# A column mean over 8192 rows: the last row group split 4, 4, 2 and 1 blocks, seven blocks loaded early, five stores

## Chip, cores and metric

One core of a Trainium2 chip. The time is device microseconds from launch to end. Before the change five runs gave a median of 628.69 us (628.66 to 628.92). The core has a matrix engine (TensorE, PE in the profile), which adds over the partitions here; a vector engine (VectorE, DVE); ScalarE (ACT) and GpSimd (POOL); and SyncE (SP), which only issues transfers and waits. Matmul results are held in PSUM, everything else in SBUF, with 128 partitions each.

## The reference

```python
def setup_inputs():
    return {
       "x": np.random.randn(8192, 8192).astype(np.float32),
    }

def reference(x: np.ndarray) -> np.ndarray:
    return np.mean(x, axis=0)
```

The input is 256 MiB of float32, the output 8192 numbers.

## The kernel before

The 8192 rows are 64 groups of 128, one row per partition. A group is 8192 columns wide, 16 blocks of 512 (`F`). The sum over the rows has two parts. First VectorE adds groups elementwise into an accumulator `acc` of 128 x 8192. Then TensorE adds over the partitions: a matmul with a 128 x 32 matrix `ones`, whose entries are 1/8192, leaves the mean of its columns in 32 partitions of PSUM, all alike. Four such matmuls write to the four quarters of a PSUM tile (partitions 0, 32, 64 and 96). Several matmuls accumulate in the same place, so that the late groups need not pass through `acc`: TensorE adds them in directly.

The buffers are six rows of one SBUF tile `bufs`. Rows 0 to 3 take loads in turn, row 4 is `both`, row 5 is `acc`. All loads are issued by SyncE in program order (line 75, in the helper `load`) and share one queue; a load into a buffer waits for the operation that last read it. `load_rows` loads several groups with one transfer.

The order is this. `head` takes 3 blocks of group 60 ahead of time and `ahead` 4 blocks of group 63. Groups 0 to 3 and 4 to 5 come in two large loads. Groups 6 to 53 come in pairs: one load for two groups, one add of the two into `both`, one add of `both` into `acc` (lines 118 to 123). Groups 54 to 59 come one by one, with one add each. Of group 60 only blocks 3 to 15 are loaded and added, of group 61 all are loaded and blocks 5 to 15 added (line 129). Group 62 is loaded, and GpSimd adds its blocks 13 to 15 to `acc` (line 136). Group 63 comes in three loads: blocks 0 to 7, 12 and 13, 14 and 15 (line 139).

An add in the helper `add` (line 95) that waits both for a load and for the add ahead of it does so through a no-op on ScalarE or GpSimd (line 98), which waits for both and releases VectorE.

The table `plan` (line 142) gives the order of the matmuls (line 169) on TensorE: `ahead`, the blocks of `acc` as they become final, the parts of groups 61, 60, 62 and 63 that are not in `acc`. The blocks 0 to 11 go to three PSUM tiles `banks`, four blocks each. Blocks 12 and 13, and 14 and 15, go in pieces of 256 columns to two smaller tiles `ends`.

Results leave PSUM by a copy to SBUF: ScalarE copies `banks[2]`, `banks[0]`, `banks[1]` and `ends[0]` (line 183), VectorE copies `ends[1]` (line 201). Four stores follow (line 186): one of blocks 8 to 11 on ScalarE's queue, one of blocks 0 to 7 on SyncE's, one of 12 and 13 on ScalarE's and one of 14 and 15 on SyncE's. The helper `landed` puts a no-op on SyncE (line 70) that waits for certain transfers, before the stores and behind them. VectorE's last no-op `hold` (line 212) waits for the store of blocks 0 to 7.

Of the kernel before, what the change touches and what calls it, by code (L numbers as in the profile page):

```python
# [9 lines left out]
def kernel(  # L10
# [32 lines left out]
    W = F // 2  # L43
    WHOLE = 12
# [11 lines left out]
    ahead = sb.tile([P, 4 * F], f32, name="ahead")  # L56
# [6 lines left out]
    banks = [psp.tile([P, F], f32, name=f"bank{b}") for b in range(3)]  # L63
    ends = [psp.tile([P, W], f32, name=f"end{e}") for e in range(2)]
# [20 lines left out]
    def rows(g, n=1):  # L85
        return x[g * P:(g + n) * P, :]
# [6 lines left out]
    def add(dst, a, b, dmas):  # L93

        ins = nc.vector.tensor_add(out=dst, in0=a, in1=b).ins  # L95
        if dmas and adds:
            waiter = nc.scalar if len(adds) % 8 > 1 else nc.gpsimd
            nop = joins[waiter] = tc.keep_in_program_order(waiter.nop()).ins  # L98
            for o in dmas + adds[-1:]:
                tc.add_manual_dep(nop, o.name, sync, reason="the no-op waits")  # L100
            for group in ("loads", "adds"):
                tc.declare_no_dep(ins, group=group, reason="the no-op waited")
            tc.add_manual_dep(ins, nop.name, sync, reason="waits for both at once")
        elif adds:
            tc.declare_no_dep(ins, group="loads", reason="the add ahead waited")
        tc.add_to_no_dep_group("adds", ins)
        adds.append(ins)

    head = sb.tile([P, 3 * F], f32, name="head")
    load(head[:], rows(G - 4)[:, :3 * F])  # L110
    first, second = load_rows(0, 0, 4), load_rows(4, 4, 2)
    load(ahead[:], rows(G - 1)[:, 8 * F:WHOLE * F])
# [3 lines left out]
    tc.keep_in_program_order(nc.scalar.copy(out=warm[:], in_=ones[:]))  # L116
    g = 6
    while g < G - 10:
        u = (g + 2) % 4
        dma = load_rows(g, u, 2)  # L120
        add(both, bufs[:, u, :], bufs[:, u + 1, :], [dma])
        add(acc, acc, both, [])
        g += 2
# [5 lines left out]
    for lo, loaded in [(3, 3), (5, 0)]:  # L129
        row = bufs[:, (g + 2) % 4, :]  # L130
        dma = load(row[:, loaded * F:], rows(g)[:, loaded * F:])
        add(acc[:, lo * F:], acc[:, lo * F:], row[:, lo * F:], [dma])
        g += 1
    r61, r62, r63 = [bufs[:, (g + 1 + j) % 4, :] for j in range(3)]
    load(r62, rows(g))
    tc.keep_in_program_order(nc.gpsimd.tensor_add(  # L136
        out=acc[:, 13 * F:], in0=acc[:, 13 * F:], in1=r62[:, 13 * F:]))
    g += 1
    for lo, hi in [(0, 8), (12, 14), (14, 16)]:
        load(r63[:, lo * F:hi * F], rows(g)[:, lo * F:hi * F])  # L140

    plan = [
        (ahead, 8, 12),
        (acc, 3, 5),
        (acc, 0, 3),
        (r61, 0, 5),
        (head, 0, 3),
        (acc, 5, 12),
        (r62, 0, 12),
        (r62, 12, 13),  # L150
        (acc, 12, 14),
        (acc, 14, 16),
        (r63, 0, 8),
        (r63, 12, 14),
        (r63, 14, 16),
    ]
    sums = []
    for row, lo, hi in plan:
        base = 8 * F if row is ahead else 0
        if lo < WHOLE:  # L160
            for i in range(lo, hi):
                cols = row[:, i * F - base:(i + 1) * F - base]
                sums.append((banks[i // 4], i % 4, cols))
        else:
            for c in range(lo * F, hi * F, W):
                e, q = divmod(c // W - 2 * WHOLE, 4)
                sums.append((ends[e], q, row[:, c:c + W]))
    for n, (dst, q, cols) in enumerate(sums):
        tc.keep_in_program_order(nc.tensor.matmul(  # L169
            out=dst[32 * q:32 * q + 32, :],  # L170
            lhsT=ones[:],
            rhs=cols,
            start=all(d is not dst or k != q for d, k, _ in sums[:n]),
            stop=all(d is not dst or k != q for d, k, _ in sums[n + 1:]),
            tile_position=(0, 32 * q),
            skip_group_check=True,
        ))

    res = both[:, :3 * F].rearrange("p (b c) -> p b c", b=3)
    tails = [both[:, 3 * F:3 * F + W], tail[:]]  # L180

    def copy(dst, src):
        tc.keep_in_program_order(nc.scalar.copy(out=dst, in_=src))  # L183
# [7 lines left out]
    def end(e):  # L191
        return (out[(WHOLE + 2 * e) * F:(WHOLE + 2 * e + 2) * F].rearrange("(q c) -> q c", q=4),
                tails[e][0:P:32, :])

    copy(res[:, 2, :], banks[2][:])
    s2 = store(nc.scalar, out[8 * F:12 * F].rearrange("(q c) -> q c", q=4), res[0:P:32, 2, :],
               loads[-3])
    for b in range(2):
        copy(res[:, b, :], banks[b][:])
    copy(tails[0], ends[0][:])  # L200
    nc.vector.tensor_copy(out=tails[1], in_=ends[1][:])  # L201
# [4 lines left out]
    s01 = store(nc.sync, out[:8 * F].rearrange("(b q c) -> q b c", b=2, q=4), res[0:P:32, 0:2, :])  # L206
    s3 = store(nc.scalar, *end(0))
    store(nc.sync, *end(1))
    landed(loads[-2], s2)
    landed(loads[-1], adds[-1])  # L210
    landed(s01, s3)
    hold = tc.keep_in_program_order(nc.vector.nop()).ins
    tc.add_manual_dep(hold, s01.name, sync, reason="VectorE ends late")
# [30 lines left out]
```

## Time and profile before

| What | us |
|---|---|
| median of 5 runs | 628.69 |
| the profiled execution, its own time | 628.67 |
| its span, first to last instruction | 626.8 |
| VectorE busy | 526.1 (84%) |
| TensorE busy | 17.5 (3%) |
| GpSimd, ScalarE busy | 4.0, 3.5 |
| load stream, over the span | 428 GB/s |
| last load landed | 623.07 |

The page has a row for each engine over the span cut into 40 slices, each digit a busy share in tenths, and a row for the sixteen transfer engines together. Groups of instructions are named by line, engine, operation and tile, with their number, busy time and mean; behind a bar stands how long the engine was idle before them and what ended that. The chain of waits follows the work that ended last back from its end. In the timeline a row gives start and length. SPq and ACTq are the sequencers of SyncE and ScalarE, where a transfer is issued. PEld is TensorE's loading of weights, and each float32 matmul shows as two records.

### The profile page before, as it was taken

The page shows a single profiled execution, that of the slowest core. Times are in us where ns is not written, and L with a number is a line of the kernel's source. Part 1 is how long each engine was busy: PE and PEld are TensorE (multiplying, and loading weights), DVE is VectorE, ACT ScalarE, POOL GpSimd, SP SyncE. Part 2 cuts the span into 40 slices and gives each one's busy share as a digit, 9 for nine tenths or more (in the row PEclk, how much of TensorE's full clock was granted, in tenths as well). Part 3 has the DMA queues.
Part 4 walks back from the last instruction along what each step waited for, and adds up shares of the span by engine and source line. Part 5 has one row for each costly group of instructions (what it writes and reads, how often), then busy time and mean ns, then how long its engine had stood idle before and what let it go on. Part 6 is the DMA issues. An engine that isn't in the chain of part 4 may idle for free.

```text
span 626.8 us, 475 instructions
## 1 busy us (share of the span) xinstructions
PE 17.5 (3%) x124; PEld 4.7 (1%) x124; DVE 526.1 (84%) x60; ACT 3.5 (1%) x6; POOL 4.0 (1%) x7
## 2 busy tenths in 40 slices
PE   0000100000000000000000000000000000000027
PEld 0000000000000000000000000000000000000002
DVE  0028999999888998888988889888898888999991
ACT  0000000000000000000000000000000000000001
POOL 0000000000000000000000000000000000000002
PEclk9999999999999999999999999999999999999999
DMA  9999999999999999999999999999999999999997
GB/s 385 460 410 412 458 452 418 443 427 435 435 418 452 402 468 402 468 402 468 402 468 402 468 402 468 402 456 414 448 422 443 427 435 412 425 435 435 439 425 294
DMA packets 5926, 268.50 MB, mean 428 GB/s; under 512 B 656, under 2 KB 664, under 8 KB 1060
## 3 DMA queue, kind: packets, MB, share of 16 engines
q1 hardware_dynamic: 5908, 268.46, 99.2%
q8 instruction: 1, 0.02, 0.0%
q10 hardware_dynamic: 16, 0.01, 0.0%
q14 instruction: 1, 0.01, 0.0%
HBM read 268.44 MB, written 0.03 MB: 428 GB/s over the span
## 4 chain that ended last, share of the span: by engine, by line
DMA 56%; DVE 33%; another core or an unknown queue 10%; issue 0%; SPq 0%; PE 0%; ACTq 0%; POOLq 0%; POOL 0%
DMA bufs<-in_x_dram 56%; DVE bufs L95 33%; SPq L75 0%; PE end L169 0%; ACTq L98 0%; DVE tail L201 0%; POOLq L98 0%; POOL ready L62 0%; POOL ones L59 0%; POOLq L228 0%
## 5 line engine op out<-in xcount | busy, mean ns | idle before, releaser
L95 DVE TENSOR_TENSOR bufs<-bufs 128x8192 f32<-128x8192 f32 (+3 forms) x59 | 525.6, 8909 | 88.0 <-DMA bufs<-in_x_dram 43.8
L169 PE MATMUL bank<-bufs,ones 128*32 128x512 f32 x74 | 11.8, 688 | 540.4 <-DVE bufs L95 539.9
L201 DVE COPY tail<-end 128x256 f32<-128x256 f32 x1 | 0.4, 425 | 10.2 <-PE end L169 10.2
L136 POOL TENSOR_TENSOR bufs<-bufs 128x1536 f32<-128x1536 f32 x1 | 3.5, 3467 | 614.7 <-DMA bufs<-in_x_dram 614.7
L169 PEld LDWEIGHTS bank<-bufs,ones 128*32 128x32 f32 x74 | 2.8, 118 | 549.8 <-DVE bufs L95 542.6
L183 ACT COPY bufs<-bank 128x512 f32<-128x512 f32 x3 | 1.8, 586 | 619.2 <-PE bank L169 619.2
L169 PE MATMUL bank<-ahead,ones 128*32 128x512 f32 x8 | 1.9, 1057 | 65.8 <-DMA ahead<-in_x_dram 65.8
L169 PE MATMUL end<-bufs,ones 128*32 128x256 f32 x36 | 3.3, 384 | 0.1
L169 PE MATMUL bank<-head,ones 128*32 128x512 f32 x6 | 1.9, 600 | 0.0
L169 PEld LDWEIGHTS end<-bufs,ones 128*32 128x32 f32 x36 | 1.4, 109 | 2.4 <-DMA bufs<-in_x_dram 0.8
L116 ACT ACT_TABLE_LOAD x1 | 1.3, 1283 | 0.7 <-PEq L228 0.7
L169 PEld LDWEIGHTS bank<-ahead,ones 128*32 128x32 f32 x8 | 0.2, 138 | 65.7 <-issue 65.7
L183 ACT COPY bufs<-end 128x256 f32<-128x256 f32 x1 | 0.4, 378 | 0.0
L169 PEld LDWEIGHTS bank<-head,ones 128*32 128x32 f32 x6 | 0.4, 108 | 0.6 <-issue 0.6
L116 ACT COPY warm<-ones 128x32 f32<-128x32 f32 x1 | 0.2, 218 | 0.0
L62 POOL TENSOR_TENSOR ready<-ones 128x1 f32<-128x1 f32 x1 | 0.2, 194 | 0.1
L59 POOL MEMSET ones<- 128x32 f32 x1 | 0.1, 125 | 0.3 <-POOLq L228 0.3
L228 POOL MEMSET const-bfloat16-1.0<- 128x1 bf16 x1 | 0.1, 103 | 0.0
L228 POOL MEMSET const-uint8-127<- 128x1 uint8 x1 | 0.1, 103 | 0.0
L228 POOL MEMSET const-float32-0.0<- 128x1 f32 x1 | 0.1, 100 | 0.2 <-issue 0.2
L228 POOL MEMSET const-float32-1.0<- 128x1 f32 x1 | 0.1, 100 | 0.0
## 6 DMA issues: line engine op xcount, KB each, us to landing
bufs<-in_x_dram SPq DMA_DIRECT2D x8, 4096.0 KB, 24.1
bufs<-in_x_dram SPq DMA_DIRECT2D x1, 3328.0 KB
bufs<-in_x_dram SPq DMA_DIRECT2D x1, 2048.0 KB, 20.2
ahead<-in_x_dram SPq DMA_DIRECT2D x1, 1024.0 KB
bufs<-in_x_dram SPq DMA_DIRECT2D x2, 512.0 KB, 21.5
head<-in_x_dram SPq DMA_DIRECT2D x1, 768.0 KB
bufs<-in_x_dram SPq DMA_DIRECT2D x26, 29.9
out_dram<-bufs ACTq DMA_DIRECT2D x1, 8.0 KB
```

The costliest lines, as they stand in the source:

```text
L59: nc.gpsimd.memset(ones[:], 1.0 / M)
L62: nc.gpsimd.tensor_add(out=ready[:], in0=ones[:, 0:1], in1=ones[:, 1:2]))
L95: ins = nc.vector.tensor_add(out=dst, in0=a, in1=b).ins
L116: tc.keep_in_program_order(nc.scalar.copy(out=warm[:], in_=ones[:]))
L136: tc.keep_in_program_order(nc.gpsimd.tensor_add(out=acc[:, 13 * F:], in0=acc[:, 13 * F:], in1=r62[:, 13 * F:]))
L169: tc.keep_in_program_order(nc.tensor.matmul(out=dst[32 * q:32 * q + 32, :], lhsT=ones[:], rhs=cols, start=all(d is not dst or k != q for d ...
L183: tc.keep_in_program_order(nc.scalar.copy(out=dst, in_=src))
L201: nc.vector.tensor_copy(out=tails[1], in_=ends[1][:])
L228: nc = _bacc.Bacc("TRN2", target_bir_lowering=False, num_devices=1)
```

## The change

- The early loads are one tile `early` of 7 blocks: blocks 9 to 13 of group 63 and blocks 14 and 15 of group 60. `head` and `ahead` go.
- GpSimd adds `early` to `acc` in two pieces, of 4 blocks after the pair at group 24 and of 3 blocks after the pair at group 32. The next add into `acc` waits for that.
- Group 60 is loaded and added in blocks 0 to 13; group 61 as before.
- GpSimd's add of group 62 becomes two: blocks 14 and 15, then block 8.
- Group 63 comes in four loads: blocks 4 to 7, 0 to 3, 14 and 15, and 8.
- PSUM has two `banks` (blocks 0 to 7), `wide` (9 to 13, as four quarters of 640 columns), `two` (14 and 15) and `last` (8, as four quarters of 128 columns).
- Five stores: 9 to 13 on ScalarE's queue, 4 to 7 and 0 to 3 on SyncE's, 14 and 15 on ScalarE's, 8 on SyncE's. `hold` waits for the store of 0 to 3.

```diff
-    W = F // 2
-    WHOLE = 12
+    W = F // 4
...
-    ahead = sb.tile([P, 4 * F], f32, name="ahead")
+    early = sb.tile([P, 7 * F], f32, name="early")
...
-    banks = [psp.tile([P, F], f32, name=f"bank{b}") for b in range(3)]
-    ends = [psp.tile([P, W], f32, name=f"end{e}") for e in range(2)]
+    banks = [psp.tile([P, F], f32, name=f"bank{b}") for b in range(2)]
+    wide = psp.tile([P, 2 * F], f32, name="wide")
+    two = psp.tile([P, 2 * W], f32, name="two")
+    last = psp.tile([P, W], f32, name="last")
...
+        tc.declare_no_dep(ins, group="early", reason="the no-op waited, or the add behind it")
...
-    head = sb.tile([P, 3 * F], f32, name="head")
-    load(head[:], rows(G - 4)[:, :3 * F])
+    load(early[:, 5 * F:], rows(G - 4)[:, 14 * F:])
     first, second = load_rows(0, 0, 4), load_rows(4, 4, 2)
-    load(ahead[:], rows(G - 1)[:, 8 * F:WHOLE * F])
+    load(early[:, :5 * F], rows(G - 1)[:, 9 * F:14 * F])
...
-        add(acc, acc, both, [])
+        add(acc, acc, both, ahead)
+        ahead = []
+        if g in (24, 32):
+            lo, hi = (0, 4) if g == 24 else (4, 7)
+            cols = slice((9 + lo) * F, (9 + hi) * F)
+            ins = tc.keep_in_program_order(nc.gpsimd.tensor_add(
+                out=acc[:, cols], in0=acc[:, cols], in1=early[:, lo * F:hi * F])).ins
+            tc.add_to_no_dep_group("early", ins)
+            ahead = [ins]
         g += 2
...
-    for lo, loaded in [(3, 3), (5, 0)]:
+    for lo, hi, loaded in [(0, 14, 14), (5, 16, 16)]:
...
-    tc.keep_in_program_order(nc.gpsimd.tensor_add(
-        out=acc[:, 13 * F:], in0=acc[:, 13 * F:], in1=r62[:, 13 * F:]))
+    for cols in [slice(14 * F, 16 * F), slice(8 * F, 9 * F)]:
+        tc.keep_in_program_order(nc.gpsimd.tensor_add(
+            out=acc[:, cols], in0=acc[:, cols], in1=r62[:, cols]))
...
-    for lo, hi in [(0, 8), (12, 14), (14, 16)]:
+    for lo, hi in [(4, 8), (0, 4), (14, 16), (8, 9)]:
         load(r63[:, lo * F:hi * F], rows(g)[:, lo * F:hi * F])
...
+    def blocks(row, lo, hi):
+        for i in range(lo, hi):
+            sums.append((banks[i // 4], i % 4, 0, row[:, i * F:(i + 1) * F]))
+
+    def spread(dst, row, lo, hi):
+        n = (hi - lo) * W
+        for c in range(0, n, F):
+            for q in range(4):
+                at = lo * F + q * n + c
+                sums.append((dst, q, c, row[:, at:at + min(F, n - c)]))
+
+    blocks(acc, 2, 5)
+    blocks(acc, 0, 2)
+    blocks(r61, 0, 5)
+    blocks(acc, 5, 8)
+    spread(wide, acc, 9, 14)
+    blocks(r62, 0, 8)
+    spread(wide, r62, 9, 14)
+    blocks(r63, 4, 8)
+    spread(two, acc, 14, 16)
+    spread(last, acc, 8, 9)
+    blocks(r63, 0, 4)
+    spread(two, r63, 14, 16)
+    spread(last, r63, 8, 9)
...
+    copy(res5, wide[:, :5 * W])
+    s5 = store(nc.scalar, part(9, 14), res5[0:P:32, :], loads[-4])
+    copy(res[:, 1, :], banks[1][:])
+    copy(res[:, 0, :], banks[0][:])
+    copy(res2, two[:])
+    nc.vector.tensor_copy(out=tail[:], in_=last[:])
     landed(*loads[-8:-6])
     landed(*loads[-6:-4])
     landed(*loads[-4:-2])
     landed(*joins.values())
-    s01 = store(nc.sync, out[:8 * F].rearrange("(b q c) -> q b c", b=2, q=4), res[0:P:32, 0:2, :])
-    s3 = store(nc.scalar, *end(0))
-    store(nc.sync, *end(1))
-    landed(loads[-2], s2)
+    s1 = store(nc.sync, part(4, 8), res[0:P:32, 1, :])
+    s0 = store(nc.sync, part(0, 4), res[0:P:32, 0, :])
+    s2 = store(nc.scalar, part(14, 16), res2[0:P:32, :])
+    store(nc.sync, part(8, 9), tail[0:P:32, :])
+    landed(loads[-2], s5)
     landed(loads[-1], adds[-1])
-    landed(s01, s3)
+    landed(s0, s1)
+    landed(s2)
     hold = tc.keep_in_program_order(nc.vector.nop()).ins
-    tc.add_manual_dep(hold, s01.name, sync, reason="VectorE ends late")
+    tc.add_manual_dep(hold, s0.name, sync, reason="VectorE ends late")
```

## The prediction

> **What bounds the kernel now.** I read the page's slices first, then the groups, then the chain of waits near the end, then the timeline of the last ten microseconds and SyncE's waits.
>
> ```profile
> span 626.8 us, 475 instructions
> DVE  0028999999888998888988889888898888999991
> DMA  9999999999999999999999999999999999999997
> HBM read 268.44 MB, written 0.03 MB: 428 GB/s over the span
> L95 DVE TENSOR_TENSOR bufs<-bufs 128x8192 f32<-128x8192 f32 (+3 forms) x59 | 525.6, 8909 | 88.0 <-DMA bufs<-in_x_dram 43.8
> ```
>
> The DMA row is at nine in every slice but the last: the load stream never stops, and 268.44 MB pass through it before and after the change. VectorE has gaps; its 84% is cover, not the bound. So only what follows the last landing can shrink, unless something breaks the stream.
>
> ```profile
> 600.31 0.33 SPq L75
> ...
> 601.16 21.91 DMA bufs<-in_x_dram
> 623.07 0.04 issue
> 623.11 0.68 PE end L169 x8
> 623.80 0.02 issue
> 623.82 0.42 DVE tail L201
> ```
>
> These are the last pieces of the chain, by start and length. The last load was issued at 601.16 and landed at 623.07, queued behind the others. Then come four last matmuls (eight records), a copy, and what the chain doesn't name: a store and the program's end, 626.8 - 624.24 = 2.6 us.
>
> ```profile
> 615.80 3.47 POOL L136 TENSOR_TENSOR bufs<-bufs 128x1536 f32<-128x1536 f32 x1 [614.67 <-DMA bufs<-in_x_dram]
> 620.64 1.08 ACTq L186 DMA_DIRECT2D out_dram<-bufs  x1
> 622.65 0.59 ACT L183 COPY bufs<-bank 128x512 f32<-128x512 f32 x1 [0.27 <-PE bank L169]
> 623.14 0.38 ACT L183 COPY bufs<-end 128x256 f32<-128x256 f32 x1
> 623.27 0.71 SPq L186 DMA_DIRECT2D out_dram<-bufs  x1
> 623.54 0.51 ACTq L186 DMA_DIRECT2D out_dram<-bufs  x1
> 623.82 0.42 DVE L201 COPY tail<-end 128x256 f32<-128x256 f32 x1 [10.21 <-PE end L169]
> 624.27 0.56 SPq L186 DMA_DIRECT2D out_dram<-tail  x1
> ```
>
> This is the timeline (start, length). SyncE issues its last store at 624.27, when VectorE's copy is done, but ScalarE's store went out only 0.73 us earlier, at 623.54.
>
> ```profile
> SPq L70 <- DMA out_dram<-bufs: 0.5, 1, 0.5
> SPq L239 <- DMA out_dram<-tail: 0.2, 1, 0.2
> ```
>
> SyncE waits first for the older stores (line 70's no-op, passed at 625.4 by that line's events), then branches at 625.6 and waits 0.2 us more for the last one, until about 625.9; the rest, 0.8 us, is the closing barrier. So two stores end nearly together: the older wait has 0.2 to 0.3 us of slack against the last store. That slack caps the gain.
>
> **The change, part by part.** The profiled execution's own time is 628.67 us: its span of 626.8 and 1.9 around it. The median of the five runs is 628.69, so the sum can be made on either.
>
> *The load stream.* Row group 60 loads 14 blocks of 512 columns where it loaded 13, the last group 11 late ones where it loaded 12; the two early loads hold 7 blocks together, as `head` and `ahead` did. Bytes are equal. There is one more load, and the smallest is 256 KB. Rows: group 62 landed at 615.80 (POOL starts), the 8-block load at 620.64, the last at 623.11: 0.61 us a block for the large one (4.84/8), 0.62 for the two small ones together (2.47/4). Two loads instead of one piece of that size thus cost 0.05 us at most. Nothing shows a 256 KB load; the bounds are 0, and 0.3 us if its one block took half as long again. I take 0.03, near the two-block rows. Landings then, counted back from 623.14 at 0.61 a block: 8:9 at 623.14, 14:16 at 622.53, 0:4 at 621.31, 4:8 at 618.87, group 62 at 616.43.
>
> *VectorE.* The add of group 60 grows by 512 columns. From 7091 ns for 6656 columns and 6026 for 5632, that is 0.53 us, so the add of group 61 ends at 614.2 instead of 613.63. Cover: group 62, which needs no VectorE, lands at 616.43. Without that cover it would cost 0.53.
>
> *GpSimd in mid-stream.* The two early adds (2048 and 1536 columns, after groups 24 and 32) have no row beside a busy VectorE. The same operation on 1536 columns alone took 3467 ns, on one column 194, so 2.13 ns a column and 4.56 us for 2048. Low bound: no delay, for VectorE idles about 1.9 us before each pair's first add and spends 8.70 on that add, so the accumulator is needed again 10.6 us later. High bound: the two engines exclude each other, and VectorE runs late by all 4.56. Cover: a pair's load lands 29.9 us after its issue, while pairs follow each other every 19.35 (38.70 for two); 10.5 us are queued at each issue, and SyncE's next issue is what waits behind VectorE. The stream breaks only past 10.5, and the 1.9 of idle time repays 4.56 in three pairs, the second add coming four later. I take zero.
>
> [...]
>
> *GpSimd at the end.* Two adds (1024 and 512 columns, 2.38 and 1.29 us by the same slope) replace one of 3.47, starting at 616.45: they end at 618.8 and 620.1. TensorE needs the second before block group 0:4 at 621.31. Cover 1.2 us.
>
> *TensorE.* The matmuls on `ahead` and `head` go; the program has 61 where it had 62, many narrower. Twelve blocks took 2.57 us from 615.78 to 618.35, 0.214 a block. Group 62 (13 blocks' worth) then takes until 619.4, r63's 4:8 until 620.2, and the rest waits for landings. The clock bears on this: matmul records of 512 columns lasted 1.06 us early in the burst that starts at 607.54 and 0.59 from about 610.9 on. After the change the burst starts at 608.1 and holds ten blocks; `acc` blocks 0 and 4, and 0 of r61 after them, share a quarter of the array and cannot overlap, so four groups at 1.71 fill the time to 614.9 at the slow rate, longer than the 3.3 us that the rise took. Later idle stretches are 1 us or less. I take the fast rate.
>
> [...]
>
> *The last piece.* From the last landing to VectorE's copy took 623.82 - 623.11 = 0.71 with 256-column matmuls. A 512-column record lasts 592 ns, a 256-column one 379, so 128 columns last about 272, and the second record follows 0.12 instead of 0.24 behind the first: 0.71 - 0.11 - 0.12 = 0.48. The copy of 128 columns: 256 took 425, and ScalarE's 587 and 378 for 512 and 256 give 0.82 ns a column, so 0.32; VectorE's slope of 1.04 would give 0.29. I take 0.30. SyncE's last store goes out at 623.14 + 0.48 + 0.30 + 0.03 = 623.95 instead of 624.27: 0.32 us earlier.
>
> *ScalarE and SyncE.* ScalarE now copies 640 columns (0.69 by its slope, 619.4 to 620.1), issues the store of blocks 9 to 13 (1.08, as its first store does now, to 621.2), copies bank 1 (to 621.8), and bank 0 when its matmuls are done: that copy began 1.16 us after its load's landing (621.80 - 620.64), so 622.47 to 623.06. SyncE issues the store of bank 1 near 621.8, of bank 0 at 623.08, 0.56 to 0.71 each, so it is free at 623.8, before 623.95. Then ScalarE copies 14:16: their matmuls are the shape that now takes 0.71, so 622.53 + 0.71 = 623.24, plus 0.38, and its store goes out at 623.64. It now goes at 623.54. **This is the new limit**: SyncE's no-op waits for that store, 0.10 later than now, and 0.06 comes back because the no-op names one store, not two. The branch comes 0.04 later, at 625.65, and the last store has landed by then. The 0.2 us wait at line 239 shrinks to the 0.17 that the branch itself takes now (625.57 to 625.74), and the next event follows in 0.02 instead of 0.19.
>
> *Sum.* Last store alone: -0.32. ScalarE's store: SyncE leaves at about 625.65 + 0.17 + 0.02 = 625.84 instead of 625.93, so -0.1. The later one rules: 628.67 - 0.1 = 628.57, rounded to 628.55.
>
> **The rivals.** *The last store rules after all.* If ScalarE's store lands as early as bank 0's, the full 0.32 is gained: 628.3. For it: bank 0 and bank 1 no longer leave SyncE just ahead of ScalarE's store, where 0.71 us of issuing overlapped it. Against it: the 625.4 wait ends long after the 623.54 issue, and that distance was not idle queueing for sure.
>
> *Slower: ScalarE's last issue.* Its first store took 1.08 us to issue, the second 0.51. If the second store takes the long form too, being 256 columns from a new place behind one of 640, SyncE's no-op ends 0.57 later and the end 0.57 - 0.1 = 0.47 after today's: 629.1. It decides once that store is issued or copied 0.1 us later than in my sum. For it: ScalarE has only 0.66 us free between bank 1's copy and bank 0's; against it: the second issue was short.
>
> *Slower: the stream breaks at group 26 or 34.* From 10.5 us of lateness on, each further microsecond is one of the total; with 12.5, 630.7. Against it: the high bound is 4.56.
>
> *Small loads cost more than the two-block rows show.* At the 0.3 bound the last landing is 623.41 and both stores follow: 628.85.
>
> **How the numbers follow.** Forecast 62%, last store rules 17%, long issue on ScalarE 11%, small loads 6%, broken stream 4%. The time is the first case's, 628.55, its own range 628.4 to 628.75. The range for eight in ten reaches to the full gain less 0.1 (628.2) and to the long issue (629.1). About 0.2%, 1.26 us, is what a measurement here can tell from no change: below 627.43 is out of reach of every case, since the whole path behind the last landing gives 0.32 (2% for what I have not seen); above 629.95 lies the broken stream, and what pushes both slow cases together (6%). Within: 92%.
>
> **What would show it.** Right: the last load released TensorE at 623.1 to 623.2, SyncE's last store at about 623.95, ScalarE's at about 623.65, SyncE waiting longer at line 70's successor and not at the end. Wrong: DMA slices under nine before the last; a VectorE wait on GpSimd of over a microsecond that ends in a load issued late; matmuls of 1.06 us after 616; ScalarE's issue at 624 or later.

## The result: 630.23 us, slower by 1.6, and the profile after

| | before | after |
|---|---|---|
| median us (lowest to highest, runs) | 628.63 (628.39 to 629.0, 45) | 630.23 (628.45 to 630.79, 25) |
| profiled execution, its span | 628.67, 626.8 | 630.27, 628.5 |
| last landing seen by TensorE | 623.11 | 624.60 |
| last store issued | 624.27 | 625.42 |

The ratio is 1.0022 (1.0016 to 1.0027). The forecast was 628.55 with a range to 629.1. The runs of the changed kernel fall into two heaps with nothing between them: 5 of 25 at 628.45 to 629.22, around the forecast, and 20 at 630.06 to 630.79. The profiled execution is of the upper heap.

The page of the changed kernel, its slices and first group:

```profile
span 628.5 us, 481 instructions
DMA  9999999999999999999999999999999999999996
HBM read 268.44 MB, written 0.03 MB: 427 GB/s over the span
L96 DVE TENSOR_TENSOR bufs<-bufs 128x8192 f32<-128x8192 f32 (+3 forms) x59 | 530.1, 8984 | 84.0 <-DMA bufs<-in_x_dram 43.0
```

The stream has no hole before the last slice, and the bytes are the same. So the time was lost at the end. The chain of waits there (start, length):

```profile
601.13 0.43 SPq L76
601.56 0.04 issue
601.60 22.95 DMA bufs<-in_x_dram
624.56 0.04 issue
624.60 0.47 PE last L181 x8
625.07 0.02 issue
625.10 0.29 DVE tail L212
```

The last load is on its way for 22.95 us where it was 21.91. The pieces behind it, 0.47 and 0.29, are short as forecast. The timeline tells which step is late:

```profile
619.43 0.69 ACT L196 COPY bufs<-wide 128x640 f32<-128x640 f32 x1 [617.19 <-PE wide L181]
620.15 1.07 ACTq L199 DMA_DIRECT2D out_dram<-bufs  x1
621.26 1.06 PE L181 MATMUL bank<-bufs,ones 128*32 128x512 f32 x8 [0.38 <-DMA bufs<-in_x_dram]
622.39 0.59 ACT L196 COPY bufs<-bank 128x512 f32<-128x512 f32 x1 [0.54 <-PE bank L181]
622.55 0.64 PE L181 MATMUL two<-bufs,ones 128*32 128x256 f32 x8 [0.22 <-DMA bufs<-in_x_dram]
623.66 0.52 ACTq L199 DMA_DIRECT2D out_dram<-bufs  x1
624.60 0.42 PE L181 MATMUL last<-bufs,ones 128*32 128x128 f32 x8 [1.41 <-DMA bufs<-in_x_dram]
625.42 0.50 SPq L199 DMA_DIRECT2D out_dram<-tail  x1
```

Blocks 0 to 3 are there at 621.26 and blocks 14 and 15 at 622.55, as forecast (621.31 and 622.53). One block later, 0.6 us of stream, the last load should follow; it is seen 2.05 us later. SyncE's waits name what is then at the end:

```profile
SPq L199 <- DVE tail L212: 1.8, 1, 1.8
SPq L252 <- DMA out_dram<-tail: 1.3, 1, 1.3
```

SyncE waits 1.3 us for the last store at the very end, where it was 0.2. From before to after the landing is 1.49 later; from there to the last store's issue it is 0.34 less (0.82 for 1.16); the store takes 2.24 us from its issue until it is seen (625.42 to 627.66) where it took 1.66 (624.27 to 625.93), 0.58 more. These make the 1.7 by which the span has grown. Two terms are new: the landing and the store.

What lies in the gap shows in the transfers of the 100 ns from 622.3 on (queue, kind: packets, MB, share of 16 engines):

```profile
q8 instruction: 1, 0.02, 68.8%
q1 hardware_dynamic: 17, 0.02, 68.4%
```

q1 is the load queue. The one packet on q8 is a fetch of instructions, 16,384 bytes in the packet record. Its share, 0.688 of 16 engines over 0.1 us, is 1.10 us on one engine: it lasts from 622.374 to 623.475. The load ahead of the last ends with 16 packets of 4 bytes in the packet record, as many as there are transfer engines, the last of them at 622.01, and TensorE sees it landed at 622.55. They are taken here for the load's semaphore, one from each engine. Of the last load's 16, fifteen are written between 622.3 and 622.67; one is missing by then. The transfers from 623.43 to 623.6 are that one alone, and before the change there is none there:

```profile
DMA  0000000300000000000000000000000000000000
DMA packets 1, 0.00 MB, mean 0 GB/s; under 512 B 1, under 2 KB 1, under 8 KB 1
q1 hardware_dynamic: 1, 0.00, 0.9%
```

It starts at 623.461, when the fetch ends, 0.8 us behind the others; and TensorE sees the landing 1.1 us after it, where a last packet is normally seen after 0.5 (0.49 in the kernel before, 0.52 in the run with 45 spare matmuls below). 0.8 and 0.6 make the 1.4 us. Why it is 1.1 here and not 0.5, no trace shows. In the profile of before, the same fetch is at 622.235 for 1.03 us (transfers of the 100 ns from 622.2 on):

```profile
q8 instruction: 1, 0.02, 64.2%
```

There all semaphore packets of the last load are written by 622.62, before the fetch ends, and none waits for it. So it is taken to lie behind its engine's semaphore, and it costs nothing that shows.

### The profile page after: what moved, and what is told of

It is laid out like the page before. It is cut to its first block, busy times and chain, and to the rows that moved or that the text cites. A ratio compares the mean times of both kernels' runs of the same rounds, so it can differ in the third digit from the quotient of the medians.

```text
span 628.5 us, 481 instructions
## 1 busy us (share of the span) xinstructions
PE 14.8 (2%) x122; PEld 4.4 (1%) x122; DVE 530.4 (84%) x60; ACT 3.7 (1%) x6; POOL 12.1 (2%) x10
## 4 chain that ended last, share of the span: by engine, by line
DMA 55%; DVE 34%; another core or an unknown queue 10%; issue 0%; SPq 0%; ACTq 0%; PE 0%; POOL 0%; POOLq 0%
DMA bufs<-in_x_dram 55%; DVE bufs L96 34%; SPq L76 0%; ACTq L99 0%; PE last L181 0%; DVE tail L212 0%; POOLq L99 0%; POOL ready L61 0%; POOL ones L58 0%; POOLq L241 0%
## 5 line engine op out<-in xcount | busy, mean ns | idle before, releaser
L129 POOL TENSOR_TENSOR bufs<-bufs,early 128x2048 f32<-128x2048 f32 (+1 forms) x2 | 7.9, 3955 | 348.4 <-DVE bufs L96 348.4
L148 POOL TENSOR_TENSOR bufs<-bufs 128x1024 f32<-128x1024 f32 (+1 forms) x2 | 3.6, 1829 | 258.9 <-DMA bufs<-in_x_dram 258.9
L181 PE MATMUL wide<-bufs,ones 128*32 128x512 f32 (+1 forms) x32 | 3.4, 433 | 0.0
L181 PEld LDWEIGHTS wide<-bufs,ones 128*32 128x32 f32 x32 | 1.3, 110 | 2.3 <-issue 2.3
L181 PE MATMUL two<-bufs,ones 128*32 128x256 f32 x16 | 1.3, 385 | 0.2 <-DMA bufs<-in_x_dram 0.2
```

The source lines that it names most:

```text
L129: ins = tc.keep_in_program_order(nc.gpsimd.tensor_add(out=acc[:, cols], in0=acc[:, cols], in1=early[:, lo * F:hi * F])).ins
L148: tc.keep_in_program_order(nc.gpsimd.tensor_add(out=acc[:, cols], in0=acc[:, cols], in1=r62[:, cols]))
L181: tc.keep_in_program_order(nc.tensor.matmul(out=dst[32 * q:32 * q + 32, c:c + cols.shape[1]], lhsT=ones[:], rhs=cols, start=all((d is dst, ...
```

## The experiments

At the start there were three theories. A: the fetch of instructions stands in the last load's way, and it is TensorE's, set off at a fixed count of its instructions (A2: counted from the start; A3: from the end of the program). B: the new small transfers, a 256 KB load and five stores, cost the time themselves. C: GpSimd's early adds put the stream late. "Spare" matmuls have 32 columns, read the matrix of ones, and their result is not used; each matmul has two matmul and two weight records. Ratios are to the kernel before on the same chip, measured along with it.

**TensorE with one matmul less, then one spare.**

```diff
-    for lo, hi, loaded in [(0, 14, 14), (5, 16, 16)]:
+    for lo, hi, loaded in [(0, 14, 14), (4, 16, 16)]:
...
-    blocks(acc, 2, 5)
+    blocks(acc, 2, 4)
     blocks(acc, 0, 2)
-    blocks(r61, 0, 5)
-    blocks(acc, 5, 8)
+    blocks(r61, 0, 4)
+    blocks(acc, 4, 8)
```

The second kernel has this and one spare matmul at the head of TensorE's work.

> The changed kernel with one matmul fewer: block 4 of group 61 is added by VectorE (its add of that group covers blocks 4 to 15) and no longer by TensorE; everything else, the small loads and the five stores too, stays. Theory A (a 16 KB fetch of instructions, set off when TensorE has issued about 218 of its weight-load and matmul records, runs on one transfer engine just ahead of the last load's semaphore there): with 4 records fewer the 218th is issued with the group on blocks 14 and 15, after 622.5, and the fetch falls at about 623.2, behind the last load. Then every run is near 628.4 to 628.6, and the last load releases TensorE at about 623.15. Theory B (a 256 KB load or a 512-byte row in a store costs more in itself) and theory C (the early adds on GpSimd or the fifth store): unchanged, a median of 630.2 with the last landing at 624.6; VectorE's add is 0.5 us longer and hidden.

> The kernel of e1 with one matmul of 32 columns, ones by ones into a spare PSUM tile, put at the head of TensorE's stream at the start of the kernel, where TensorE idles for 600 us. Nothing reads it. Theory A: the count of records is that of the changed kernel again, the fetch is back at about 622.4 and most runs are near 630.2. Theories B and C, or a gain in e1 by VectorE's longer add: the same time as e1.

Measured: 629.59 (629.27 to 630.79), ratio 1.0018 (1.0009 to 1.0026); and 629.5 (629.17 to 631.06), 1.002 (1.0011 to 1.0029). A was not borne out as stated, and the edit had a second effect. TensorE's first burst is shorter, TensorE is idle for 3.0 us before 614.61, and its matmuls are slow afterwards. Windows of the second kernel (sum; PE, PEld, DVE, ACT, POOL busy; granted clock; DMA share; GB/s):

```profile
612.00:614.00 2.00, 0.00 (x0) 0.00 (x0) 2.00 (x1) 0.00 (x0) 0.00 (x0) 1.00 0.65 279
616.00:618.00 2.00, 2.00 (x20) 0.85 (x16) 0.00 (x0) 0.00 (x0) 1.70 (x1) 0.50 1.01 422
618.00:620.00 2.00, 2.00 (x20) 0.49 (x15) 0.00 (x0) 0.00 (x0) 1.88 (x2) 0.75 1.01 422
```

The granted clock is at 0.50 from 615.6 to 619.0, and the work for the banks came late. So these two say nothing on the fetch in the changed kernel, but for one figure: in the first, whose matmuls are slow, the fetch comes at 623.04, with all loads landed, and TensorE is then at its 164th matmul or weight record. What asks for it is at or before that one, unless TensorE's sequencer was by then ahead of the record that ran. In the kernel before, weight loads of 607.57 to 607.60 belong to matmuls of 608.39, so it can be ahead by 0.8 us; by how much it was here, no run shows.

**The kernel before, with one spare matmul at the head.** The spare is the loop shown further down, with one turn.

> The kernel before with the same spare matmul of 32 columns at the head of TensorE's stream, and no other edit. Theory A: the 218th record is issued 0.43 us earlier, at about 621.15, so the fetch starts at about 621.8, among the last load's packets on one transfer engine; that engine ends later and its semaphore with it: 629.2 to 630.3 instead of 628.65. Theories B and C: 628.6, as before, for the loads, stores and adds are those of the kernel before.

628.68 (628.57 to 628.93), ratio 1.0 (0.9991 to 1.0009); the fetch is at 622.41, behind the semaphore. A in its first form fails: one matmul more does not bring the kernel before into the upper heap.

**No early adds.** This leaves seven blocks out of the sum.

```diff
-        if g in (24, 32):
+        if g in ():
```

> The changed kernel without GpSimd's two early adds: the seven early blocks are loaded and not added, so that part of the sum is left out. Theory A: still 630.2 in most runs, with the last landing near 624.6. Theory C (the adds in mid-stream cost the time): 628.4 to 628.6.

630.25 (630.17 to 630.55), ratio 1.0025 (1.0016 to 1.0034), as slow as with them. C is out. What the adds did in mid-stream is seen by VectorE's adds of 8192 columns, first with and then without them:

```profile
L96 DVE TENSOR_TENSOR bufs<-bufs 128x8192 f32<-128x8192 f32 x55 | 482.0, 8763 | 38.6 <-ACTq L99 28.5 <-POOLq L99 8.2
```

```profile
L96 DVE TENSOR_TENSOR bufs<-bufs 128x8192 f32<-128x8192 f32 x55 | 478.1, 8692 | 42.4 <-ACTq L99 29.0 <-POOLq L99 11.7
```

VectorE lost 3.9 us, and its idle time shrank by as much.

**Four matmuls less.** Blocks 9 to 13 of group 62 lose the last 128 columns of each quarter; all loads, stores and adds stay.

```diff
     spread(wide, r62, 9, 14)
+    del sums[-4:]
```

> The changed kernel without the four matmuls of 128 columns that take group 62 into the last quarter of each part of wide; that part of the sum is left out. Every load, store, copy and add of the changed kernel stays, and TensorE's first burst from 608 us is the same, so its clock rises as there. The first form of theory A, a fixed count of executed records, fell with e1 to e3. Its second form, A2: the 16 KB fetch follows about 1.05 us after TensorE's sequencer, which runs ahead of the array until a wait stops it, gets to a certain place near the end of its stream (in the changed kernel that is set free by the load of blocks 0 to 3 at 621.26, so 622.37). With 16 records fewer ahead of it the place lies behind the wait for blocks 14 and 15 (622.55), the fetch comes at about 623.6, and every run is at 628.3 to 628.7 with the last landing seen at 623.15. If the place is some 12 records earlier than I think, it stays with blocks 0 to 3 and the time at 630.2. Theory B (256 KB load, 512-byte rows of the store): 630.2. A theory that has the fetch set off by another engine or by the clock: 630.2.

628.25 in the median, 628.15 to 628.52 in all 11 runs, ratio 0.9994 (0.9985 to 1.0002). The upper heap is gone, with every small transfer still there: B is out. The fetch lies at 622.67, behind the semaphore, and not at 623.6 as A2 had it.

**The last load in two, in the kernel before.** Blocks 14 and 15 come in two loads of 256 KB.

```diff
-    for lo, hi in [(0, 8), (12, 14), (14, 16)]:
+    for lo, hi in [(0, 8), (12, 14), (14, 15), (15, 16)]:
...
-        (r63, 14, 16),
+        (r63, 14, 15),
+        (r63, 15, 16),
...
```

> The kernel before with its last load (blocks 14 and 15, 512 KB) split into two of 256 KB; the matmuls, stores and adds stay, so this is the small load alone. Theory B (a 256 KB load costs more in itself): 629.5 to 630.2. Theory A: the small load costs 0.05 us, and the time is 628.65 unless the fetch comes in ahead of a semaphore here too, which the load's 2 KB packets may allow; then it is 629.7 to 630.2 in some runs, and the trace shows the 16 KB fetch ahead of the late landing.

628.57 (628.45 to 628.95), ratio 0.9999 (0.9991 to 1.0008). A 256 KB load at the end costs nothing that shows.

**The last two loads swapped, in the changed kernel.** Block 8 comes ahead of 14 and 15, and TensorE takes them in that order.

```diff
-    for lo, hi in [(4, 8), (0, 4), (14, 16), (8, 9)]:
+    for lo, hi in [(4, 8), (0, 4), (8, 9), (14, 16)]:
...
```

> The changed kernel with its last two loads, and their matmuls, in the other order: block 8 (256 KB) first, then blocks 14 and 15 (512 KB) last. If it is the small last load that lets the fetch in ahead of the semaphore (packets of 2 KB, 0.66 us in all on each engine, against 1.27 us for packets of 4 KB as in the kernel before): near 628.6, every run. If only the moment of the fetch counts: 630.2 in most runs, as now.

630.5 (628.91 to 631.01, one of eight below 630), ratio 1.0027 (1.0017 to 1.0037). The size of the last load is not it either.

**Four and eight spare matmuls at the head, four at the end.**

```diff
+    for _ in range(4):
+        tc.keep_in_program_order(nc.tensor.matmul(
+            out=spare[0:32, :], lhsT=ones[:], rhs=ones[:], start=True, stop=True,
+            tile_position=(0, 0), skip_group_check=True))
     for n, (dst, q, c, cols) in enumerate(sums):
```

The kernel with eight has `hold` on the store of blocks 14 and 15 as well. In the third the loop stands behind the matmuls.

> The changed kernel with four spare matmuls of 32 columns (ones by ones, into a PSUM tile that nothing reads) at the head of TensorE's stream, at the start of the kernel. Theory A2: the place is reached 16 records sooner, before the wait for blocks 0 to 3, once the matmuls on acc's block 8 are let go near 620.1; the fetch then reaches its transfer engine at about 621.2, while loads still pass. As in the kernel before, where TensorE is let go at 620.64, it would be served with some 0.5 us and more of loads behind it or wait for them: either 628.5 (the engine's other work hides it) or 629.3 and more (the engine ends 0.5 to 1 us late). A time other than 630.2 speaks for A2 either way. Theory B and a fetch set off by another engine: 630.2 with the fetch at 622.4.

> Both edits together, with eight spare matmuls instead of four: TensorE's place is reached 32 records sooner, with the matmuls that wait for nothing after 618.9 but the load of blocks 4 to 7, so the fetch comes near 620.2; VectorE's no-op waits for the later store. Theory A2: if an early fetch is hidden, 628.3 to 628.6, the time that the changed kernel was meant to have; if it pushes its engine's loads back, 629 to 629.7 (0.5 us less than with four spares, by the hold). Theory B: 630.2.

> The changed kernel with four spare matmuls (32 columns, ones by ones into a PSUM tile that nothing reads) at the end of TensorE's stream instead of at its head. In the runs so far the 16 KB fetch comes 1.0 to 1.2 us after TensorE is let go by the load of blocks 0 to 3, however many records stand ahead of that (the changed kernel, and those with 16 fewer, 16 and 32 more), and that is 32 to 48 records from the end of the stream. Theory A3: the fetch is set off when the stream's end is that near. With 16 records more behind, the point moves to the wait for blocks 14 and 15 at 622.5, the fetch to about 623.6, behind the last load's semaphores (622.3 to 622.7): 628.2 to 628.6 in every run, the same loads, stores and adds notwithstanding. Theory A4 (the fetch is not tied to TensorE's place, the kernel with four matmuls less was quick by another order of events): 630.2 in most runs with the fetch near 622.4. Theory B (the 256 KB load, 512-byte rows): 630.2.

With four 630.37 (3 of 10 runs at 628.45 to 628.73), with eight 630.36 (5 of 12 at 628.22 to 628.81), with four at the end 628.41 (7 of 12 at 628.17 to 628.51, the others at 630.05 to 630.37); ratios 1.0019 (1.001 to 1.0028), 1.0014 (1.0005 to 1.0023) and 1.0008 (0.9999 to 1.0017). The fetch is at 622.88, 622.32 and 622.06. Sixteen or thirty-two records move it neither earlier nor later: A2 and A3 fall. The heaps stay, and only their sizes change.

What parts the heaps shows in the profiled executions. In nine of them a last semaphore packet follows the end of the fetch or comes with it: the changed kernel, the one without early adds, the swapped loads, four and eight spares at the head, and below 24 spares, one store and the two with another `hold`. These took 629.93 to 630.92 us. In six no semaphore packet of the last load follows it: the kernel before, with one spare and with two small loads, the four matmuls less, four spares at the end, and the last experiment below. These took 628.17 to 628.71. The other five profiles are late in other ways, told at their places.

**Forty-five and twenty-four spare matmuls at the head.** If the fetch is TensorE's at all, enough of them must move it past the place where it waits.

> The changed kernel with 45 spare matmuls of 32 columns on the matrix of ones in front of TensorE's own, while TensorE has nothing else to do; their result is not used. If the 16 KB instruction fetch on queue q8 at 622.37 belongs to TensorE and goes by the number of instructions behind it, 90 more records move it: it comes at the start of the kernel or in the burst at 608, no fetch on q8 lies between 620 and 624, the last landing is seen at 623.1 to 623.4, and the time is 628.0 to 628.6 in every run. If it belongs to another engine or goes by the distance from the end, it stays at 622.1 to 622.9 and the median at 629.9 to 630.5.

> The changed kernel with 24 spare matmuls of 32 columns in front of TensorE's own. If the fetch is TensorE's and goes by the number of instructions behind it, 48 more records bring it some 10 us forward, into the burst at 608 to 614 where the load queue is full; it then delays no last semaphore, the last landing is seen at 623.1 to 623.4 and the time is 628.0 to 628.6. If it only comes when the load queue of its transfer engine is about empty, however early it was asked for, it stays at 622.1 to 622.9, and the runs fall partly at 628.3 to 628.8 and partly at 630.0 to 630.6, as with 4 and 8 spares.

With 45: 629.27, in one heap from 629.08 to 629.76, ratio 1.0011 (1.0002 to 1.0019). From 620 on there is no fetch on q8. It is at 8.54 us; transfers of the 200 ns from 8.4 on:

```profile
q1 hardware_dynamic: 4, 0.26, 302.3%
q8 instruction: 1, 0.02, 29.2%
```

So the fetch is TensorE's. The time was expected at 628.0 to 628.6, and this missed: the fetch in mid-stream was not free here. Its share is 0.93 us of one engine, and at the end of the stream one engine still works after the others have done. Windows of this kernel, columns as above:

```profile
622.90:623.10 0.20, 0.20 (x8) 0.00 (x0) 0.00 (x0) 0.03 (x1) 0.00 (x0) 1.00 0.09 31
623.10:623.30 0.20, 0.20 (x4) 0.00 (x0) 0.00 (x0) 0.00 (x0) 0.00 (x0) 1.00 0.08 31
623.30:623.50 0.20, 0.10 (x4) 0.00 (x0) 0.00 (x0) 0.03 (x1) 0.00 (x0) 1.00 0.05 20
623.50:623.70 0.20, 0.10 (x4) 0.10 (x8) 0.00 (x0) 0.20 (x1) 0.00 (x0) 1.00 0.06 20
```

A DMA share near 0.06 is one engine of sixteen. Its last semaphore is at 623.67, 1.0 us behind most of the others', and the landing is seen at 624.19, 1.05 after the forecast. If each engine writes one of a load's sixteen semaphore packets, as taken above, what one of them loses early is lost at the load's end. The packet record names the queue and not the engine, so that the late engine is the one with the fetch is inferred, from 0.93 us of fetch and 1.0 us of lateness.

With 24: 630.18 (629.49 to 630.89), ratio 1.0023 (1.0014 to 1.0033). The fetch is at 622.42, though TensorE had passed its 164th record at 615.0. If it was asked for by then, as the first experiment suggests, it waited 7.4 us, until the load stream was at its end; no run shows the moment of asking, nor what it waited for.

**One store for blocks 0 to 7.**

```diff
-    s1 = store(nc.sync, part(4, 8), res[0:P:32, 1, :])
-    s0 = store(nc.sync, part(0, 4), res[0:P:32, 0, :])
+    s0 = store(nc.sync, out[:8 * F].rearrange("(b q c) -> q b c", b=2, q=4), res[0:P:32, 0:2, :])
...
-    landed(s0, s1)
+    landed(s0)
```

> The changed kernel with one store on SyncE for blocks 0 to 7, as before the change, where it has two; four stores in all. If the store that SyncE issues at 621.9, while the load stream still runs, is what lets the 16 KB fetch in ahead of the last load's semaphore, that store is gone here: the fetch starts after the semaphores, the last landing is seen at 623.1 to 623.4 and the time is 628.3 to 628.9. If it has nothing to do with it, the fetch stays ahead, the landing is seen at about 624.5, and the median is 629.9 to 630.5.

630.39 (3 of 12 at 628.08 to 628.5, the others 630.1 to 631.31), ratio 1.0021 (1.0011 to 1.003). The store issued during the stream does not let the fetch in.

**The last store's own 0.55 us.** After VectorE's last instruction an 8 KB fetch follows on queue q14, at 626.26 for 0.49 us. Three of the last store's four packets go out at 626.56 to 626.59, the fourth at 626.74, when the fetch ends; the store is seen 0.9 us after the semaphore behind it. The two kernels here move VectorE's end, by the transfer that its last no-op `hold` waits for.

```diff
-    tc.add_manual_dep(hold, s0.name, sync, reason="VectorE ends late")
+    tc.add_manual_dep(hold, s2.name, sync, reason="VectorE ends late")
```

The second kernel puts the store of block 8 there.

> The changed kernel with VectorE's last no-op waiting for ScalarE's store of blocks 14 and 15 instead of SyncE's store of blocks 0 to 3; nothing else. In the changed kernel VectorE ends at 625.7, a fetch of 8 KB starts 0.55 us later on one transfer engine, at 626.26, just ahead of the last store's packets there, and SyncE sees that store at 627.66, 2.24 us after its issue where the kernel before takes 1.66. Theory A2: this second fetch moves behind the last store and the slow runs fall by about 0.5 us, from 630.2 to 629.7; the last landing stays at 624.6. Theory B (512-byte rows make the store slow): the store still takes 2.2 us and the time stays at 630.2.

> The changed kernel with VectorE's last no-op waiting for the last store itself, so that VectorE ends after that store has landed. The hold on ScalarE's store moved VectorE's end too little, for that store lands at 625.5, as VectorE's late copy ends. Theory: in the changed kernel the fetch of 8 KB that follows VectorE's end by 0.5 to 0.8 us runs ahead of the last store on one engine and adds 0.55 us to its landing. Now the store lands 1.6 to 1.7 us after its issue instead of 2.24; VectorE's end comes behind it, about 0.6 us, so the time itself changes little: 630.0 to 630.4 in the disturbed runs. If 512-byte rows made the store slow it would still take 2.2 us, and the time would grow to 630.8.

With the store of 14 and 15: 630.38 (630.29 to 630.89), ratio 1.0028 (1.0017 to 1.0039); that store ends too early to move VectorE's end much, and the last store still takes 2.7 us. With the last store itself: 629.98 (628.56 to 630.39), ratio 1.002 (1.0012 to 1.0029). There the last landing is late too, at 624.44, but the store takes 1.58 us (625.25 to 626.83) and is seen 0.35 us after its last semaphore, and the fetch on q14 follows at 627.98. SyncE's wait for it:

```profile
SPq L252 <- DMA out_dram<-tail: 0.6, 1, 0.6
```

0.6 where it was 1.3. So the second term is the same thing at a smaller scale: a fetch by an engine, ahead of a semaphore. The median is 0.25 us below that of the changed kernel, but the intervals of the two ratios overlap, so what comes back of the 0.55 is not shown; SyncE waits 0.7 us in the closing barrier there, for VectorE's late end.

**Group 62 on VectorE**, to have fewer TensorE instructions and the whole sum.

```diff
-    for cols in [slice(14 * F, 16 * F), slice(8 * F, 9 * F)]:
-        tc.keep_in_program_order(nc.gpsimd.tensor_add(
+    for cols in [slice(9 * F, 14 * F), slice(14 * F, 16 * F), slice(8 * F, 9 * F)]:
+        tc.keep_in_program_order(nc.vector.tensor_add(
...
-    spread(wide, acc, 9, 14)
     blocks(r62, 0, 8)
-    spread(wide, r62, 9, 14)
+    spread(wide, acc, 9, 14)
```

> The changed kernel with blocks 8 to 15 of group 62 added by VectorE, in three pieces (9 to 13, then 14 and 15, then 8), where TensorE took blocks 9 to 13 and GpSimd the others. TensorE has eight matmuls less, 212 matmul and weight records instead of 244. VectorE is done with group 61 at 614.2; the pieces are 2560, 1024 and 512 columns at 1.04 ns, 4.3 us in all, so from 616.45 to about 620.8, ahead of TensorE's use of blocks 14, 15 and 8. If the fetch goes by TensorE's count, it comes later against the stream and lies behind the last load's semaphore, as with the four matmuls left out: last landing seen at 623.1 to 623.4, last store at 623.9 to 624.2, and 628.1 to 628.5 in every run. If the count has no part in it, the runs spread over 628.4 to 630.8 as in the changed kernel, with a median near 630.2.

> The same kernel, and VectorE's last no-op waits for the store of block 8 in place of the store of blocks 0 to 3. If VectorE's end draws the 8 KB fetch that delays the last store, the store takes 1.6 us from issue to being seen: 0 to 0.5 us less than with the no-op on blocks 0 to 3, so 627.9 to 628.4. If not, the two kernels agree within 0.2 us.

629.46 (629.2 to 629.84), ratio 1.0013 (1.0005 to 1.0022), and 629.57 (629.34 to 629.75), 1.0014 (1.0005 to 1.0023). The fetch on q8 does come later, at 623.43 and 623.64, and the two heaps are gone; but 628.5 was not reached. The two agree within 0.11 us, the outcome given for a VectorE whose end draws no fetch. It fits: in both the 8 KB fetch ran earlier (620.14 and 620.38), and none follows VectorE's end within the span. The transfers of the 100 ns from 620.1 on, in the first of the two:

```profile
q1 hardware_dynamic: 3, 0.02, 58.4%
q14 instruction: 1, 0.01, 20.6%
```

VectorE's three more adds bring its own 8 KB fetch, which came after its end, forward into the stream at 620.14 (0.206 of 16 engines over 0.1 us: 0.33 us). A packet of 8 KB at 620.46 then lasts 0.97 us, the load's last packets on one engine run at 623.01 to 623.65, and TensorE sees the last landing at 624.15. It looks like a third case of one cause, with another engine's instructions; that the fetch, the long packet and the late packets share an engine is inferred.

**The same four matmuls less as above, with the whole sum**: GpSimd adds their columns.

```diff
...
+    acc4, r62_4 = [r[:, 9 * F:14 * F].rearrange("p (q n) -> p q n", q=4)[:, :, F:] for r in (acc, r62)]
+    tc.keep_in_program_order(nc.gpsimd.tensor_add(out=acc4, in0=acc4, in1=r62_4))
     for cols in [slice(14 * F, 16 * F), slice(8 * F, 9 * F)]:
...
-    spread(wide, acc, 9, 14)
+    spread(wide, acc, 9, 14, (0,))
     blocks(r62, 0, 8)
-    spread(wide, r62, 9, 14)
+    spread(wide, r62, 9, 14, (0,))
+    spread(wide, acc, 9, 14, (F,))
     blocks(r63, 4, 8)
     spread(two, acc, 14, 16)
-    spread(last, acc, 8, 9)
     blocks(r63, 0, 4)
+    spread(last, acc, 8, 9)
```

The new argument of `spread` names the column offsets that it takes.

> The changed kernel with the 128-column ends of the four quarters of blocks 9 to 13 of group 62 added to acc by GpSimd, ahead of its two other adds, where TensorE took them: the four matmuls that were left out in an earlier run, now with the whole sum. TensorE has 228 matmul and weight records instead of 244, VectorE the same instructions. GpSimd's adds end at 617.8, 620.1 and 621.4, each before TensorE needs it. If TensorE's count sets where the 16 KB fetch lies, it lies behind the last load's semaphore, the last landing is seen at 623.1 to 623.5 and every run gives 628.1 to 628.6, below the kernel before. If the four matmuls' columns or work made the difference there, or the count has no part in it, the runs spread over 628.4 to 630.8 with a median near 630.2.

628.67, in one heap from 628.43 to 628.9, ratio 1.0001 (0.9992 to 1.001). The fetch is at 622.55, behind the semaphore, and the chain's end is:

```profile
623.30 0.45 PE last L184 x8
623.75 0.02 issue
623.77 0.29 DVE tail L215
```

SyncE's waits there, from 622 on, name the older stores and not the last one:

```profile
SPq L202 <- ACT bufs L199: 0.7, 2, 0.4
SPq L71 <- DMA out_dram<-bufs: 0.7, 2, 0.5
SPq L202 <- DVE tail L215: 0.4, 1, 0.4
SPq L255 <- PEq L255: 0.3, 2, 0.2
```

The change's loads, early adds and stores are all in this kernel, and its time is the forecast's within 0.12 us. It is as fast as the kernel before, not faster, and no version that computes the whole sum was shown to be faster: the lowest median, 628.41 with four spares at the end, goes with a ratio of 1.0008, for five of its twelve runs lie in the upper heap. Taking four matmuls from TensorE takes the loss away, as it did where they were left out; adding four or eight does not. Why the fetch is nearly always ahead of the semaphore in the changed kernel, and was behind in the profiles of the kernel before, where TensorE passes its 164th record at about the same time (619.33 against 619.63), stays open.

## Why the prediction was wrong, by its steps

- **The load stream.** The failed step is the last landing, "counted back from 623.14 at 0.61 a block: 8:9 at 623.14". It was seen at 624.60, 1.46 us late, because the last of its sixteen semaphore packets came at 623.461, as a fetch of TensorE's instructions ended. The step beside it, "Two loads instead of one piece of that size thus cost 0.05 us at most", held: blocks 0 to 3, and 14 and 15, were there within 0.05 us of the forecast, and two 256 KB loads in the kernel before gave a ratio of 0.9999. The forecast counted the bytes of q1 alone and put everything else on the sixteen engines at nothing, without a reason, though the page of before lists it:

```profile
q8 instruction: 1, 0.02, 0.0%
q14 instruction: 1, 0.01, 0.0%
```

The change of the matmuls was priced as TensorE time alone. Four matmuls less put the fetch behind the semaphore again; which part of the change had brought it ahead stays open.
- **The last store.** "SyncE's last store goes out at ... 623.95" was 625.42, wholly by the landing. That it takes as long as before was not said but used; it took 0.55 us more, since VectorE now ends just ahead of it and its fetch falls on it. The prediction named `hold` and did not ask what VectorE's end draws.
- **VectorE, group 60.** 7625 ns for 7168 columns against 7091: the 0.53 us forecast, hidden as said.
- **GpSimd in mid-stream.** Right for the reason given. VectorE's adds beside it were 2.49 and 1.42 us longer, nearly the 2.63 and 1.57 us for which they overlapped, while GpSimd's took 4.49 and 3.42 us as forecast. Overlap was nearly total exclusion here, at VectorE's cost: it lost nine tenths of it. Without the adds the time was the same.
- **GpSimd at the end, TensorE, the last piece, ScalarE.** GpSimd's adds took 2.38 and 1.28 us and ended at 620.02; the granted clock was 1.00 behind 614; the last piece took 0.50 (0.48 forecast) and the copy 0.29 (0.30). ScalarE's copies and stores lay within 0.1 us of the forecast throughout, its second store at 623.66 and in the short form, 0.52. The rival with the long form did not come. That blocks in one quarter do not overlap shows in the kernel before: by the program's order, the matmul records of the first quarter start 0.85 us apart up to 610.11 and 0.43 from 610.86 on, while the first ones of the four quarters start within 0.03.
- **The new limit.** In the profiled execution the late last store hides it. In the last experiment SyncE waits 0.7 us in two steps for the older stores and not for the last one, as forecast. But the sum carried over the 1.9 us from ScalarE's issue (623.54) to the end of that wait (625.4). It is 1.62 now: 623.76 to 625.38 there, and 623.61 to 625.23 with four spares at the end. So the rival "If ScalarE's store lands as early as bank 0's" came in part. Four spares at the end suggest what this is worth: the seven lower runs of that kernel took 628.17 to 628.51. In the last experiment SyncE sees the last store at 625.72, 0.21 us ahead of the kernel before, and loses it in the closing barrier: a step of SyncE (a drain) comes 0.47 us after the semaphore ahead of it, where it was 0.09. Both kernels with group 62 on VectorE show the same 0.47 to 0.49; what delays it is not shown.
- **The rivals and the range.** The slower rivals put a broken stream at GpSimd's early adds and up to 0.3 us on the small loads; neither came. None was a transfer that isn't the kernel's own, so the range ended at 629.1. Slower by more than 0.2% was given 6 in 100, for a broken stream or several mishaps; the ratio's interval, 1.0016 to 1.0027, lies on both sides of that bound. The cause is one that none of the cases held.

## What to carry to other kernels

Where a kernel is bound by a stream over all sixteen transfer engines, list the instruction queues in the transfer section with the loads: here a 16 KB fetch of 1.10 us went with a last semaphore packet 0.8 us behind the others, one of 0.93 us in mid-stream with packets 1.0 us behind, and the whole load was late with them. Look where each fetch lies against the last semaphore packets, before and after an edit that adds or removes instructions. Its place was not foretold here by counting instructions: four, eight and 24 more left it at the end of the stream. Free was only a fetch that no semaphore packet of the last load followed (628.17 to 628.71 us in six profiles), and two heaps in the times went with one that lay close to the last of them.

## What the runs showed of the hardware

- A fetch of 16,384 bytes for TensorE, one packet on q8, took 1.03 us on one transfer engine in the kernel before, 1.10 in the changed kernel and 0.93 with 45 spares. It came well after TensorE's 164th record while loads were queued: at 8.54 us with that record passed at 4.8, and at 622.42 with it passed at 615.0. When it was asked for, no run shows.
- The fetch on q14 was 8 KB and took 0.49 us behind VectorE's end in the changed kernel and 0.33 us in mid-stream with group 62 on VectorE. It is taken for VectorE's, for it moved with VectorE's end, from 626.26 to 627.98, when `hold` was put on the last store.
- TensorE's fetch cost nothing that shows in the kernel before; against the landing forecast for 623.14 it cost 1.05 us with 45 spares and 1.46 us in the changed kernel.
- In the kernel with block 4 on VectorE and one spare, TensorE's clock fell to 0.50 at 615.6, 1.0 us after the end of an idle stretch of 3.0 us, and stayed there for 3.4 us.
